# A diffusion-transformer layer on one core: x added by an accumulating DMA, token tiles 0 and 1 transposed together, narrow weight buffers in the down projection

## The chip, the cores and the metric

The kernel runs on one core of one Trainium2 chip. The metric is the device time of one execution in microseconds (us). Fewer is better.

## What is computed

One layer over 512 latent tokens of width 2048: a token mixer (mLSTM heads and differential attention heads, with 256 context tokens), its output projection, a normalised and gated residual, a modulated norm, and a gated feed-forward network of width 5632 with a width-3 convolution over the tokens. Cut to the part around the change:

```python
y_lat = jnp.concatenate([m_lat, d_lat], axis=-1) @ w_out[l]
x = x + ga1 * rmsnorm(y_lat, g_post_mix[l])

h_lat = modulate(rmsnorm(x, g_pre_ffn[l]), sh2, sc2)      # h * (1 + sc2) + sh2
x = x + ga2 * rmsnorm(conv_ffn(h_lat, w_up[l], conv_ffn_w[l], conv_ffn_b[l], w_down[l]), g_post_ffn[l])

def conv_ffn(h, w_up, conv_w, conv_b, w_down):
    u = dwconv3(h @ w_up, conv_w, conv_b)
    gate, val = jnp.split(u, 2, axis=-1)
    return (jax.nn.silu(gate) * val) @ w_down
```

## The kernel before

All data are float32. For TensorE each operand is split into a rounded high part and a low remainder (`split`: ScalarE casts the high part, VectorE subtracts), and each product is three matmuls (high by high, low by high, high by low). Weights come by DMA from SyncE's queue into `raw` tiles of 128x1024 (pool of three) and are split from there, either into "narrow" tiles `whi`/`wlo` of 128x512 (a pool of four of each, which is one block of weights) or into "wide" tiles `vhi`/`vlo` of 128x1024 (two of each, again one block).

The order of every engine is written out in the program and kept by the engine; nothing is chosen at run time. Where work is interleaved (deferred steps, generators), the builder's code sets that order.

**Output projection.** `phase_out_1` runs three of four groups of 512 input features with `nat_group`: for each block of 512 output columns (`cc`) the weights are split once, and four token tiles (`tt`) are multiplied by them. One `nat_unit` is one token tile by one block: 12 matmuls into one of two PSUM tiles named `nat`, then VectorE adds it into `y[tt][cc]` (L899). The fourth group is `nat_last`: all four blocks are split ahead, and token tile after token tile is finished. Behind each unit comes `each` (the sum of squares of y on ScalarE, L925, and the product with the gate row on VectorE, L978), behind each token tile comes `post`: sum, `pow` on GpSimd (L189), then y * rs + x (L990, x was loaded into a `raw` tile by L988 on SyncE's queue), the sum of squares of that (L925), the write of x to DRAM (`x1_d`, L992 on GpSimd's queue, 256 KB each), a second sum and `pow`, and the scaling by it (L997 on ScalarE, L999 on VectorE). In the trace the input tensor x appears as `in_xn`, the tiles as `xn`, and the DRAM tensor as `x_d`.

**Transposes and forms.** Token tile after token tile, four blocks of 128x128 are transposed on TensorE into one PSUM tile (`xt`, L71), shifted and scaled into `hf` by ScalarE (L1032, 128x128 each), and split into the operands of a Strassen-like up projection. Tiles 0 and 1 give the forms `A11` and `A12` (`put_form`, casts and subtractions on VectorE, L1065 and L1068); tiles 2 and 3 give `S1` to `S4` and `A22` (`sums`). `hf` of tiles 0 and 1 lies in tiles named `F` (five of them), which also hold up weights that are added by an accumulating DMA from GpSimd (`forms`, L1099). The transposes of the first two tiles stand between the last units of the output projection on TensorE where their data come in time.

**Up loop.** 44 steps `f`, each seven products of the Strassen form, with `up_first` of the first two steps among the transposes.

**Down projection.** 11 groups of four input blocks by four column blocks `cc`, again with `nat_group`. With `down=True` odd `cc` take the wide tiles and even `cc` the narrow ones, so that a block's weights can be split while the other pool's are in use. In each even `cc`, `step(64)` runs a piece of the modulation vectors for the second residual: two loads of 512 KB (`wmB`, L262) into `raw` tiles, and four VectorE operations on `macc` (L267, L269).

Of the kernel before, what the change touches and what calls it, by code (L numbers as in the profile page):

```python
# [58 lines left out]
class Prog:  # L59
# [40 lines left out]
    def load_w(self, src, n, act=False, wide=False):  # L100
# [4 lines left out]
        if wide:  # L105
            for j in range(n // 1024):
                raw = self.p_raw.tile([P, 1024], F32, tag="raw", name="raw")
                self.nc.sync.dma_start(raw, src[:, j * 1024:(j + 1) * 1024])
                hi, lo = self.wide_w()
                self.split(hi, lo, raw)  # L110
                for q in range(2):
                    his.append(hi[:, q * 512:(q + 1) * 512])
                    los.append(lo[:, q * 512:(q + 1) * 512])
            n = 0
# [786 lines left out]
    def nat_group(self, wsrc, acts, y, first, pool, tag, down=False):  # L901

        for cc in range(4):
            get = self.load_w(wsrc(cc), 2048, wide=down and cc % 2 == 1)
            if down and cc % 2 == 0:
                self.step(64)
            for tt in range(4):
                self.nat_unit(get, acts, tt, y, cc, first, pool, tag)
# [59 lines left out]
    def phase_out(self):  # L968
# [7 lines left out]
        def each(tt, cc):  # L976
            self.stat(ssy[tt], cc, y[tt][cc])
            nc.vector.tensor_tensor(y[tt][cc], y[tt][cc], rows[cc], ALU.mult)  # L978

        def post(tt):  # L980
# [3 lines left out]
            for cc in range(4):  # L984
                cs = slice(cc * 512, (cc + 1) * 512)
                if cc % 2 == 0:
                    x2 = self.p_raw.tile([P, 1024], F32, tag="raw", name="xn")
                    nc.sync.dma_start(x2, I["xn"][tt, :, cc * 512:(cc + 2) * 512])  # L988
                xn = x2[:, cc % 2 * 512:(cc % 2 + 1) * 512]
                nc.vector.scalar_tensor_tensor(xn, y[tt][cc], r, xn, ALU.mult, ALU.add)  # L990
                self.stat(ss, cc, xn)
                nc.gpsimd.dma_start(self.x1_d[tt, :, cs], xn)  # L992
                xs.append(xn)
            r2 = self.stat_done(ss)
# [11 lines left out]
        for n in ("A11", "A12", "A22"):  # L1006
            self.fm[n] = [[self.slot(n, F32R) for _ in range(4)] for _ in range(2)]
        hf = {}
        for tt in range(4):
# [3 lines left out]
            for cc in (0, 2, 1, 3):  # L1013
                if cc:
                    pt = self.ps_sm.tile([P, 512], F32, tag="sm", name="xt")
                else:
                    pt = self.ps_big.tile([P, 1024], F32, tag="big", name="xt")[:, :512]
                for j in range(4):
                    self.tr(pt[:, j * P:(j + 1) * P], y[tt][cc][:, j * P:(j + 1) * P], self.ident)
                if tt >= 2:  # L1020
                    h = self.u_tile("hf")
# [331 lines left out]
```

## Time and profile before

| what | value |
|---|---|
| time, median of 3 runs | 2743.49 us (2741.33 to 2744.75) |
| the profiled execution's own time | 2743.7 us |
| its span in the profile | 2741.9 us |
| TensorE busy | 2652.5 us, 97% of the span |
| VectorE busy | 1887.8 us, 69% |
| ScalarE busy | 1192.8 us, 44% |
| GpSimd busy | 178.6 us, 7% |
| bytes moved by DMA | 458.24 MB, 167 GB/s over the span |

The profile is of one execution; its times are microseconds from the start of the span. Busy time of an engine leaves out its waits and its DMA issues. In a row of the timeline the last bracket is the idle time before the instruction on its engine and what ended it; a row with x3 merges three alike, and its duration goes from the first's start to the last's end.

### The profile page before, as it was taken

To read this page: it belongs to the slowest core of one execution; us is meant where nothing else is said; L and a number is where in the kernel's file an instruction comes from. 1 tells how busy PE (TensorE), PEld (TensorE's weight loads), DVE (VectorE), ACT (ScalarE), POOL (GpSimd) and SP (SyncE) were. 2 spreads that over 40 slices of the span, in tenths; PEclk is the share of its full clock that TensorE was granted. 3 is DMA by queue.
4 is the path that set the end of the run, shared out by engine and by line. 5 is a ranking of instruction groups with operands and counts; after the bars stand their busy time and mean duration, and the time that the engine had idled before them with its cause. 6 is when DMAs were issued, how large, how long until landed. Compare 5 with 4: busy or idle time off the path is not lost.

```text
span 2741.9 us, 43239 instructions
## 1 busy us (share of the span) xinstructions
PE 2652.5 (97%) x16916; PEld 2355.4 (86%) x16916; DVE 1887.8 (69%) x3252; ACT 1192.8 (44%) x2185; POOL 178.6 (7%) x233
## 2 busy tenths in 40 slices
PE   6999999999999999999699999999999999999998
PEld 3678899888788888877699999999999988888786
DVE  6585867766656666546877777777777775666556
ACT  4242444434434343524755555555555563222222
POOL 0000000000000000001111111111111100000000
PEclk9999999999999999999899999999999999999999
DMA  8775434433433434344487777777777764544434
GB/s 280 273 242 196 133 117 138 138 110 115 125 136 100 154 109 132 100 139 154 131 226 197 202 193 200 192 205 196 200 197 199 204 220 159 176 160 142 135 106 151
DMA packets 139358, 458.24 MB, mean 167 GB/s; under 512 B 15936, under 2 KB 16352, under 8 KB 139152
## 3 DMA queue, kind: packets, MB, share of 16 engines
q1 hardware_dynamic: 119312, 386.64, 43.0%
q0 software_dynamic: 19840, 68.83, 11.8%
q8 instruction: 133, 2.18, 0.3%
q14 instruction: 73, 0.60, 0.1%
HBM read 429.10 MB, written 26.30 MB: 166 GB/s over the span
## 4 chain that ended last, share of the span: by engine, by line
PE 49%; DVE 1%; ACT 1%; DMA 1%; issue 0%; DVEq 0%; POOLq 0%; POOL 0%; ACTq 0%
PE up L68 31%; PE nat L68 18%; ACT hf L1032 1%; DMA raw<-in_wu 0%; DMA raw<-in_wmB 0%; DVE S L1068 0%; DVE vlo L144 0%; ACT junk L925 0%; ACT vhi L143 0%; DVE wlo L144 0%; PE xt L71 0%; PE modr L68 0%; ACT S L1067 0%; DVE A L1068 0%; DVE v L588 0%
## 5 line engine op out<-in xcount | busy, mean ns | idle before, releaser
L143 ACT CAST whi<-raw 128x512 fp32r<-128x512 f32 x492 | 302.8, 620 | 455.4 <-PE nat L68 174.6
L144 DVE TENSOR_TENSOR wlo<-raw,whi 128x512 fp32r<-128x512 f32 x492 | 337.4, 692 | 105.9 <-ACT whi L143 99.0
L68 PE MATMUL mm<-lhi,whi 128*128 128x512 f32 x912 | 373.5, 410 | 2.3 <-ACT whi L143 1.9
L68 PE MATMUL mm<-llo,whi 128*128 128x512 f32 x912 | 359.8, 395 | 0.0
L68 PE MATMUL mm<-lhi,wlo 128*128 128x512 f32 x912 | 359.8, 395 | 0.0
L68 PE MATMUL up<-S,whi 128*128 128x256 f32 x1408 | 259.3, 284 | 5.4 <-ACT S L1067 3.1
L269 DVE SCALAR_TENSOR_TENSOR macc<-raw,c,macc 128x512 f32<-128x512 f32 x240 | 179.6, 748 | 119.4 <-DMA raw<-in_wmB 116.9
L68 PE MATMUL up<-S,vhi 128*128 128x256 f32 x1408 | 253.8, 281 | 1.0 <-ACT val L1166 0.9
L899 DVE TENSOR_TENSOR y<-nat,y 128x512 f32<-128x512 f32 x208 | 142.8, 688 | 133.5 <-PE nat L68 132.6
L68 PEld LDWEIGHTS up<-S,whi 128*128 128x128 f32 x1408 | 220.0, 192 | 6.1 <-ACT S L1067 3.3
L68 PEld LDWEIGHTS up<-S,vhi 128*128 128x128 f32 x1408 | 215.5, 188 | 1.5 <-ACT val L1166 1.1
L68 PEld LDWEIGHTS mm<-lhi,whi 128*128 128x128 f32 x912 | 173.4, 190 | 41.1 <-issue 10.3
L68 PEld LDWEIGHTS mm<-lhi,wlo 128*128 128x128 f32 x912 | 172.3, 189 | 42.0 <-issue 3.3
L68 PE MATMUL up<-S,wlo 128*128 128x256 f32 x704 | 200.1, 284 | 2.3 <-DVE wlo L144 2.3
L68 PE MATMUL cx<-chl,whi 128*128 128x256 f32 x1056 | 199.4, 287 | 2.7 <-ACT vt L627 1.5
L68 PEld LDWEIGHTS mm<-llo,whi 128*128 128x128 f32 x912 | 173.0, 190 | 30.3 <-issue 3.4
L143 ACT CAST vhi<-raw 128x1024 fp32r<-128x1024 f32 x106 | 111.3, 1050 | 199.8 <-PE nat L68 154.8
L68 PE MATMUL up<-S,vlo 128*128 128x256 f32 x704 | 197.0, 280 | 0.0
L68 PE MATMUL up<-A,vhi 128*128 128x256 f32 x1056 | 192.9, 283 | 0.1
L68 PE MATMUL up<-A,whi 128*128 128x256 f32 x1056 | 192.8, 283 | 0.0
L68 PEld LDWEIGHTS cx<-chl,whi 128*128 128x128 f32 x1056 | 169.5, 192 | 10.1 <-ACT vt L627 2.4
L144 DVE TENSOR_TENSOR vlo<-raw,vhi 128x1024 fp32r<-128x1024 f32 x106 | 129.6, 1223 | 53.8 <-ACT vhi L143 53.6
(349 smaller groups left out, 5903.0 us busy)
## 6 DMA issues: line engine op xcount, KB each, us to landing
raw<-in_wu SPq DMA_DIRECT2D x132, 512.0 KB, 5.3
raw<-in_wmB SPq DMA_DIRECT2D x128, 512.0 KB, 3.9
raw<-in_w SPq DMA_DIRECT2D x105, 512.0 KB, 4.1
F<-in_wu SPq DMA_DIRECT2D x88, 512.0 KB, 5.0
F<-in_wu POOLq DMA_DIRECT2D x88, 512.0 KB, 7.6
raw<-in_wd SPq DMA_DIRECT2D x88, 512.0 KB, 4.5
mraw<-in_wmA SPq DMA_DIRECT2D x64, 512.0 KB, 5.7
raw<-in_wo SPq DMA_DIRECT2D x32, 512.0 KB, 4.0
```

The lines of the kernel that those rows point to most:

```text
L68: return self.pe(self.nc.tensor.matmul(*a, **k))
L143: self.nc.scalar.copy(hi, src)
L144: self.nc.vector.tensor_tensor(lo, src, hi.bitcast(F32), ALU.subtract)
L269: nc.vector.scalar_tensor_tensor(acc, r, c, acc, ALU.mult, ALU.add)
L899: nc.vector.tensor_tensor(y[tt][cc], ps, y[tt][cc], ALU.add)
L1032: nc.scalar.activation(h[:, js], pt[:, js], AF.Identity, bias=sh, scale=sc)
```

## The change

Three edits:

- For token tiles 0 to 2, `each` no longer multiplies y by the gate row; `post` does y * rs * row in one VectorE operation (L987 after) into the `raw` tile, a DMA from GpSimd's queue adds x to it in SBUF (L990 after, 512 KB each, two for a token tile), the sums of squares follow, and x is written to DRAM in 512 KB pieces (L993 after). Token tile 3 keeps the loads of x and the old arithmetic (L985 after).
- Token tiles 0 and 1 are transposed into shared PSUM tiles, block by block, after the last unit of the output projection. The shift takes 128x256 (both tiles at once), and the high parts of `A11` and `A12` are cast by ScalarE, 128x512 each, the low parts subtracted by VectorE, 128x512 each.
- `load_w` loses its wide form; the down projection uses the narrow tiles for every `cc`.

```diff
--- before.py
+++ after.py
@@ -97,21 +97,11 @@
     def slot(self, name, dt=F32):
         return self.p_slot.tile([P, 512], dt, tag="slot", name=name)
 
-    def load_w(self, src, n, act=False, wide=False):
+    def load_w(self, src, n, act=False):
 
         his, los = [], []
         if act:
             bh, bl = self.act("wact"), self.act("wact")
-        if wide:
-            for j in range(n // 1024):
-                raw = self.p_raw.tile([P, 1024], F32, tag="raw", name="raw")
-                self.nc.sync.dma_start(raw, src[:, j * 1024:(j + 1) * 1024])
-                hi, lo = self.wide_w()
-                self.split(hi, lo, raw)
-                for q in range(2):
-                    his.append(hi[:, q * 512:(q + 1) * 512])
-                    los.append(lo[:, q * 512:(q + 1) * 512])
-            n = 0
         for j in range(n // 512):
             if j % 2 == 0:
                 w = min(1024, n - j * 512)
@@ -901,7 +891,7 @@
     def nat_group(self, wsrc, acts, y, first, pool, tag, down=False):
 
         for cc in range(4):
-            get = self.load_w(wsrc(cc), 2048, wide=down and cc % 2 == 1)
+            get = self.load_w(wsrc(cc), 2048)
             if down and cc % 2 == 0:
                 self.step(64)
             for tt in range(4):
@@ -975,22 +965,32 @@
 
         def each(tt, cc):
             self.stat(ssy[tt], cc, y[tt][cc])
-            nc.vector.tensor_tensor(y[tt][cc], y[tt][cc], rows[cc], ALU.mult)
+            if tt == 3:
+                nc.vector.tensor_tensor(y[tt][cc], y[tt][cc], rows[cc], ALU.mult)
 
         def post(tt):
             r = self.stat_done(ssy[tt])
             ss = self.p_s.tile([P, 4], F32, tag="ssx", name="ssx")
             xs = []
             for cc in range(4):
-                cs = slice(cc * 512, (cc + 1) * 512)
                 if cc % 2 == 0:
                     x2 = self.p_raw.tile([P, 1024], F32, tag="raw", name="xn")
-                    nc.sync.dma_start(x2, I["xn"][tt, :, cc * 512:(cc + 2) * 512])
+                    ds = slice(cc * 512, (cc + 2) * 512)
+                    xd = I["xn"][tt, :, ds]
+                    if tt == 3:
+                        nc.sync.dma_start(x2, xd)
                 xn = x2[:, cc % 2 * 512:(cc % 2 + 1) * 512]
-                nc.vector.scalar_tensor_tensor(xn, y[tt][cc], r, xn, ALU.mult, ALU.add)
-                self.stat(ss, cc, xn)
-                nc.gpsimd.dma_start(self.x1_d[tt, :, cs], xn)
                 xs.append(xn)
+                if tt == 3:
+                    nc.vector.scalar_tensor_tensor(xn, y[tt][cc], r, xn, ALU.mult, ALU.add)
+                else:
+                    nc.vector.scalar_tensor_tensor(xn, y[tt][cc], r, rows[cc], ALU.mult, ALU.mult)
+                if cc % 2:
+                    if tt < 3:
+                        nc.gpsimd.dma_start(x2, xd, accum_op=ALU.add)
+                    for k in (cc - 1, cc):
+                        self.stat(ss, k, xs[k])
+                    nc.gpsimd.dma_start(self.x1_d[tt, :, ds], x2)
             r2 = self.stat_done(ss)
             for cc in range(4):
                 if cc % 2:
@@ -1005,35 +1005,44 @@
         self.fm = {}
         for n in ("A11", "A12", "A22"):
             self.fm[n] = [[self.slot(n, F32R) for _ in range(4)] for _ in range(2)]
+        def tr4(parts, name):
+            if name:
+                pt = self.ps_sm.tile([P, 512], F32, tag="sm", name="xt")
+            else:
+                pt = self.ps_big.tile([P, 1024], F32, tag="big", name="xt")[:, :512]
+            for j, (tt, cc, q) in enumerate(parts):
+                self.tr(pt[:, j * P:(j + 1) * P], y[tt][cc][:, q * P:(q + 1) * P], self.ident)
+            return pt
+
+        def shift(dst, src, k):
+            nc.scalar.activation(dst, src, AF.Identity, bias=self.mcol[:, 16 + k:17 + k],
+                                 scale=self.mcol[:, 32 + k:33 + k])
+
+
         hf = {}
-        for tt in range(4):
+        for cc in range(4):
+            h = self.f_tile("hf")
+            for half in range(2):
+                pt = tr4([(t, cc, 2 * half + q) for q in range(2) for t in range(2)], cc * 2 + half & 3)
+                for q in range(2):
+                    k = 2 * half + q
+                    shift(h[:, k * 256:(k + 1) * 256], pt[:, q * 256:(q + 1) * 256], cc * 4 + k)
+                hi, lo = (t[cc % 2 * 2 + half] for t in self.fm["A11" if cc < 2 else "A12"])
+                self.split(hi, lo, h[:, half * 512:(half + 1) * 512])
+            for tt in range(2):
+                hf[tt, cc] = h.rearrange("p (k t) -> p k t", t=256)[:, :, tt * P:(tt + 1) * P]
+        for tt in (2, 3):
             if tt == 2:
                 for n in ("S1", "S2", "S3", "S4"):
                     self.fm[n] = [self.act(n) for _ in range(2)]
             for cc in (0, 2, 1, 3):
-                if cc:
-                    pt = self.ps_sm.tile([P, 512], F32, tag="sm", name="xt")
-                else:
-                    pt = self.ps_big.tile([P, 1024], F32, tag="big", name="xt")[:, :512]
-                for j in range(4):
-                    self.tr(pt[:, j * P:(j + 1) * P], y[tt][cc][:, j * P:(j + 1) * P], self.ident)
-                if tt >= 2:
-                    h = self.u_tile("hf")
-                elif cc < 2:
-                    h2 = self.f_tile("hf")
-                    h = h2[:, :512]
-                else:
-                    h = h2[:, 512:]
-                hf[tt, cc] = h
-                for j in range(4):
-                    k = cc * 4 + j
-                    js = slice(j * P, (j + 1) * P)
-                    sh, sc = self.mcol[:, 16 + k:17 + k], self.mcol[:, 32 + k:33 + k]
-                    nc.scalar.activation(h[:, js], pt[:, js], AF.Identity, bias=sh, scale=sc)
-                if tt < 2:
-                    self.put_form("A11" if cc < 2 else "A12", cc % 2, tt, h, True)
-            if tt >= 2:
-                self.sums(tt, hf)
+                pt = tr4([(tt, cc, q) for q in range(4)], cc)
+                h = self.u_tile("hf")
+                for q in range(4):
+                    js = slice(q * P, (q + 1) * P)
+                    shift(h[:, js], pt[:, js], cc * 4 + q)
+                hf[tt, cc] = h.rearrange("p (k t) -> p k t", t=P)
+            self.sums(tt, hf)
             if tt == 2:
                 self.early = [self.up_first(0)]
             if tt == 3:
@@ -1050,7 +1059,7 @@
     def put_form(self, n, c, tt, src, on_dve=False):
 
         nc = self.nc
-        h3 = src.rearrange("p (a b) -> p a b", b=P)
+        h3 = src
         t0 = tt % 2 * P
         hi, lo = self.fm[n]
         if n[0] == "S":
@@ -1071,7 +1080,7 @@
         tt_ = self.nc.vector.tensor_tensor
         s1 = []
         for c in range(2):
-            s = self.slot("s1")
+            s = self.slot("s1").rearrange("p (k t) -> p k t", t=P)
             s1.append(s)
             tt_(s, hf[tt, c], hf[tt, c + 2], ALU.subtract)
             self.put_form("S1", c, tt, s, True)
```

How this moves instructions is shown at three places, in the order in which the engine takes them (the name of an instruction's output, `<-`, its inputs, and the shape; x3 stands for three alike in a row). Lines are those of the kernel in question; the changed kernel's are about ten lower.

GpSimd, at the end of the output projection, token tile 0 and the start of tile 1. `rs` is the small tile that `pow` works on. Before:

```order
L189 TENSOR_TENSOR rs_11974<-rs_11974,mhalf 128x1
L992 DMA x_d<-xn 128x512 x4
L189 TENSOR_TENSOR rs_11999<-rs_11999,mhalf 128x1
L189 TENSOR_TENSOR rs_12075<-rs_12075,mhalf 128x1
L992 DMA x_d<-xn 128x512 x4
```

And in the changed kernel:

```order
L179 TENSOR_TENSOR rs_11970<-rs_11970,mhalf 128x1
L990 DMA xn<-in_xn 128x1024 x2
L993 DMA x_d<-xn 128x1024 x2
L179 TENSOR_TENSOR rs_11993<-rs_11993,mhalf 128x1
L179 TENSOR_TENSOR rs_12065<-rs_12065,mhalf 128x1
```

The two accumulating loads stand between a token tile's first `pow` and its second, and the writes of x stand behind them.

VectorE, at the same place, token tile 1 and the first unit of tile 3. `ssx` holds the sums of squares of x, `ss` those of y. Before:

```order
L932 TENSOR_REDUCE rs_12075<-ss_11833 128x1
L188 TENSOR_SCALAR rs_12075<-rs_12075 128x1
L990 SCALAR_TENSOR_TENSOR xn<-y,rs_12075,xn 128x512 x4
L899 TENSOR_TENSOR y<-nat,y 128x512 x2
L932 TENSOR_REDUCE rs_12100<-ssx 128x1
L978 TENSOR_TENSOR y<-y,row 128x512
L188 TENSOR_SCALAR rs_12100<-rs_12100 128x1
L999 TENSOR_SCALAR y<-xn,rs_12100 128x512 x2
```

And in the changed kernel:

```order
L987 SCALAR_TENSOR_TENSOR xn<-y,rs_12065,row 128x512 x4
L889 TENSOR_TENSOR y<-nat,y 128x512 x3
L922 TENSOR_REDUCE rs_12088<-ssx 128x1
L178 TENSOR_SCALAR rs_12088<-rs_12088 128x1
L999 TENSOR_SCALAR y<-xn,rs_12088 128x512 x2
L889 TENSOR_TENSOR y<-nat,y 128x512
L922 TENSOR_REDUCE rs_12160<-ss_11834 128x1
```

The sum over `ssx`, which now comes after the accumulating loads, stands ahead of the sum over the next tile's `ss`, as it did before; one more unit's addition has moved ahead of it, and the products with the row are gone.

VectorE, in the down projection, about two blocks `cc`. `wlo` and `vlo` are the low parts of narrow and wide weights, `macc` the modulation piece, `glo` the low part of the next group's activations. Before:

```order
L899 TENSOR_TENSOR y<-nat,y 128x512
L269 SCALAR_TENSOR_TENSOR macc<-raw,c_95,macc 128x512
L899 TENSOR_TENSOR y<-nat,y 128x512
L269 SCALAR_TENSOR_TENSOR macc<-raw,c_95,macc 128x512
L144 TENSOR_TENSOR wlo<-raw,whi 128x512 x3
L899 TENSOR_TENSOR y<-nat,y 128x512
L144 TENSOR_TENSOR wlo<-raw,whi 128x512
L269 SCALAR_TENSOR_TENSOR macc<-raw,c_95,macc 128x512
L899 TENSOR_TENSOR y<-nat,y 128x512
L269 SCALAR_TENSOR_TENSOR macc<-raw,c_95,macc 128x512
L899 TENSOR_TENSOR y<-nat,y 128x512 x2
L144 TENSOR_TENSOR vlo<-raw,vhi 128x1024
```

And in the changed kernel:

```order
L134 TENSOR_TENSOR wlo<-raw,whi 128x512 x3
L889 TENSOR_TENSOR y<-nat,y 128x512
L134 TENSOR_TENSOR wlo<-raw,whi 128x512
L889 TENSOR_TENSOR y<-nat,y 128x512
L259 SCALAR_TENSOR_TENSOR macc<-raw,c_95,macc 128x512
L889 TENSOR_TENSOR y<-nat,y 128x512
L259 SCALAR_TENSOR_TENSOR macc<-raw,c_95,macc 128x512
L889 TENSOR_TENSOR y<-nat,y 128x512
L134 TENSOR_TENSOR wlo<-raw,whi 128x512 x2
L259 SCALAR_TENSOR_TENSOR macc<-raw,c_95,macc 128x512
L889 TENSOR_TENSOR y<-nat,y 128x512
L134 TENSOR_TENSOR wlo<-raw,whi 128x512 x2
```

The wide rows are gone, and in every second block a `macc` operation stands between the second and the third `wlo`.

## Rows read from the trace of the kernel before

**Rows 1.** Busy time by stage; columns: stretch, length, five engines, TensorE clock, DMA, GB/s.

```profile
1195.00:1255.00 60.00, 60.00 (x266) 49.47 (x265) 29.57 (x45) 14.55 (x24) 0.00 (x0) 1.00 0.28 90
1268.00:1316.40 48.40, 45.84 (x205) 37.21 (x204) 36.51 (x69) 29.24 (x76) 10.41 (x18) 1.00 0.48 167
1316.40:1371.00 54.60, 34.62 (x204) 30.67 (x202) 51.04 (x106) 43.45 (x105) 6.22 (x9) 0.75 0.41 116
2235.00:2700.00 465.00, 460.63 (x2008) 374.87 (x2007) 271.18 (x379) 127.21 (x178) 1.06 (x2) 1.00 0.46 152
```

**Rows 2.** Who waited for whom, 1255 to 1375; columns: total us, times, longest.

```profile
PE xt L71 <- ACT hf L1032: 13.9, 8, 5.7
```

**Rows 3.** Timeline of VectorE at the end of the output projection.

```profile
1281.40 0.15 DVE L932 TENSOR_REDUCE rs<-ss 128x1 f32<-128x4 f32 x1
...
1282.43 2.74 DVE L990 SCALAR_TENSOR_TENSOR xn<-y,rs,xn 128x512 f32<-128x512 f32 x4 [0.69 <-POOL rs L189]
...
1318.20 0.69 DVE L978 TENSOR_TENSOR y<-y,row 128x512 f32<-128x512 f32 x1 [0.98 <-ACT junk L925]
...
1319.88 2.74 DVE L990 SCALAR_TENSOR_TENSOR xn<-y,rs,xn 128x512 f32<-128x512 f32 x4 [0.72 <-POOL rs L189]
```

**Rows 4.** Timeline of ScalarE at the same place and behind it.

```profile
1283.21 0.63 ACT L925 ACTIVATE junk<-xn 128x512 f32<-128x512 f32 x1 [2.46 <-DVE xn L990]
1283.75 0.19 ACT L925 ACTIVATION_READ_ACCUMULATOR junk<-xn 128x1 f32 x1
...
1288.39 1.34 ACT L997 ACTIVATE y<-xn,rs 128x512 f32<-128x512 f32 x2 [1.24 <-POOL rs L189]
...
1326.20 4.63 ACT L1032 ACTIVATE hf<-xt,mcol 128x128 f32<-128x128 f32 x13
1330.66 1.11 ACT L143 CAST vhi<-raw 128x1024 fp32r<-128x1024 f32 x1
...
1344.63 1.21 ACT L1067 CAST S<-s 128x512 fp32r<-128x512 f32 x2
```

**Rows 5.** DMA issues of the whole span; last column: median us to landing.

```profile
raw<-in_wmB SPq DMA_DIRECT2D x128, 512.0 KB, 3.9
...
F<-in_wu SPq DMA_DIRECT2D x88, 512.0 KB, 5.0
F<-in_wu POOLq DMA_DIRECT2D x88, 512.0 KB, 7.6
```

**Rows 6.** DMA issues from 1160 to 1330, same columns.

```profile
xn<-in_xn SPq DMA_DIRECT2D x8, 512.0 KB, 4.4
...
F<-in_wu POOLq DMA_DIRECT2D x2, 512.0 KB, 10.0
```

**Rows 7.** Timeline of VectorE: a block change in the output projection, then one in the down projection.

```profile
1221.96 2.05 DVE L144 TENSOR_TENSOR wlo<-raw,whi 128x512 fp32r<-128x512 f32 x3 [0.64 <-ACT whi L143]
...
2314.85 1.37 DVE L144 TENSOR_TENSOR wlo<-raw,whi 128x512 fp32r<-128x512 f32 x2 [0.65 <-ACT whi L143]
2316.90 0.75 DVE L269 SCALAR_TENSOR_TENSOR macc<-raw,c,macc 128x512 f32<-128x512 f32 x1 [0.68 <-DMA raw<-in_wmB]
...
2318.17 1.28 DVE L144 TENSOR_TENSOR wlo<-raw,whi 128x512 fp32r<-128x512 f32 x2
```

**Rows 8.** Timeline of SyncE's queue, then of VectorE, in the down projection.

```profile
2420.63 0.33 SPq L262 DMA_DIRECT2D raw<-in_wmB  x1
...
2426.18 0.75 DVE L269 SCALAR_TENSOR_TENSOR macc<-raw,c,macc 128x512 f32<-128x512 f32 x1 [3.17 <-DMA raw<-in_wmB]
```

**Rows 9.** Timeline of TensorE: two idle stretches of about two us.

```profile
2238.11 0.51 PE L68 MATMUL nat<-whi,ghi 128*128 128x512 f32 x1 [1.69 <-ACT whi L143]
...
2575.43 0.28 PE L71 MATMUL modr<-tabs,mcol 128*16 128x128 f32 x1 [2.08 <-DVE mcol L286]
```

**Rows 10.** Busy time by stretch behind these two; columns as in rows 1.

```profile
2576.00:2579.50 3.50, 3.50 (x10) 2.74 (x9) 0.02 (x1) 0.00 (x0) 0.52 (x1) 0.53 0.58 183
2239.00:2243.00 4.00, 3.79 (x16) 2.99 (x17) 4.00 (x7) 2.73 (x4) 0.00 (x0) 1.00 0.55 201
```

## The prediction, made before the changed kernel was run

> **What bounds the kernel now.** I read the busy time by stage first. In the output projection up to its last group and in the down projection TensorE is busy in 60.00 of 60.00 us and in 460.63 of 465 us [rows 1]: nothing else costs time there as long as its work stays beside the matmuls. In the last group (1268 to 1316) it is busy in 45.84 of 48.40 us, so the finishing of token tiles on the other engines just keeps up. Only from 1316.4 to 1371 does TensorE stand idle, 20 of 54.6 us, with the clock at 0.75 on the mean and VectorE busy in 51.04 us. The waits of TensorE name the main releaser there: ScalarE's shift `hf`, 13.9 us [rows 2]. So the change touches three places: a stage that just keeps up, a stage that is bound by VectorE and ScalarE, and a stage that is bound by TensorE alone. 0.2% of the time, 5.5 us, is about what a measurement can tell from no change.
>
> **The end of the output projection.** Before, token tile t starts its y * rs + x operation at 1282.43 for the first and at 1319.88 for the last [rows 3]: 37.45 us for three tiles, 12.5 each, set mostly by the matmuls.
>
> Removed: 12 products with the row at 0.69 us [rows 3], 8.3 us of VectorE, six loads of x on SyncE's queue, and the many 256 KB writes on GpSimd's queue become eight of 512 KB. Before, these products lie beside matmuls (all but the one ahead of each sum), so I cost the removal at 0.5 us once, at the first tile. The freed SyncE queue makes weights arrive earlier, which nobody waits for.
>
> Added: the statistics of x wait until the accumulating load has landed. Behind that wait stand, on ScalarE, the statistics of the next tile's y, and on VectorE the sum over `ssx`, the scaling, and only then the next tile's last addition and its sum. Both engines keep their order, so the load's whole landing time enters the chain from one tile to the next, which becomes: four y * rs * row operations, 2.74 us [rows 3]; the landing of the second load; the two statistics that hang on it, 2 x 0.73 us (0.63 and the read of the sum, which ends 0.73 behind the start [rows 4]); reduction, `pow` and scaling until the next operation starts, 1.03 us (from 1281.40 to 1282.43 [rows 3]); two scalings on ScalarE, 1.34 us, that stand ahead of the next tile's remaining statistics [rows 4]; three of these, 2.19 us; and 1.03 us again for sum and `pow`. Without the landing this is 9.8 us.
>
> The landing has no row of its own. The nearest is the same kind of DMA of the same size, on the same queue: the accumulating load of up weights, 7.6 us by its median over the span [rows 5]. A plain load to the same tiles lands in 5.0 us, one of x in 4.4 us, and the two accumulating loads just ahead of this place took 10.0 us [rows 5, 6]. I take 7.6, for this is a median of 88 with a second load beside it as here, and keep 5.0 and 10.0 as ends. The Trainium skill prices the queue at less: "DMA: Bandwidth & Descriptors", section "SWDGE vs HWDGE vs iDMA" and its table of specifications, give about 1 us to the first byte from GpSimd's queue and about 0.6 us from SyncE's, 0.4 apart; the load of x would then land in about 4.8 us (an estimate from that page and the row of x), and the sum below would be 8 us smaller. The rows have 2.6 us between the two queues for the same bytes, and they decide.
>
> So a tile takes 9.8 + 7.6 = 17.4 us, and three take 52.2 instead of 37.45: the last tile starts 14.7 us later, plus about 0.7 for its four products in a row, minus the 0.5 above: **+15 us** (+7 at a landing of 5.0, +22 at 10.0). TensorE cannot fill this: it has two PSUM tiles, and their additions wait on VectorE in the same order. GpSimd's second `pow` waits behind the writes of x, which wait for the same landing and issue while ScalarE does its statistics; costed at 0. SyncE's weight loads are early.
>
> **Transposes and forms.** Before, ScalarE needs from 1319.88 to 1330.66, 10.8 us, until it casts the first up weight [rows 3, 4]. On this way the change puts six casts of 128x512 that VectorE did before, 0.6 us each from the row of two in 1.21 [rows 4], 3.6 us; eight shifts of 128x256 and eight of 128x128 stand where there were sixteen of 128x128 at 4.63 / 13 = 0.36 us [rows 4], about 0.1 more for each of the wide ones, 0.8 us. Some 1.4 us of the casts fit into the wait for the last `pow`. Net **+3 us**. VectorE loses some 5 us of casts in this stage, and it is the busier engine; but it now waits for ScalarE's casts, and its list behind the first up weight is the same within a few us. I cost that at 0 with 5 us either way. What is saved by the joint shift (sixteen calls instead of 32) lies mostly in the wait for the loads, where it is worth nothing.
>
> **The down projection.** Without the wide pool, a block's weights can be cast only as the last token tile of the block before releases them, one after the other. That alone is what the output projection does at each block, at full TensorE busy [rows 1]; there three `wlo` take 2.05 us in one go [rows 7], which is the pace of the matmuls (266 matmuls began in those 60 us, so the 12 of a unit take 2.71 us for four pieces of the weights). So most block changes cost nothing. But at 13 of the 44 blocks the new order has a `macc` operation and an addition between the second and the third `wlo`, and that `macc` waits for the load of its second piece. This pattern stands twice in the order before, and one of them can be read: two `wlo` from 2314.85 to 2316.22, then 0.68 us of waiting for the `wmB` load, the `macc` at 2316.90, an addition, and the other two at 2318.17 [rows 7]. In one go the third would have started at about 2316.1, so it is 2.07 us late. Before, this is covered, for TensorE is then on a wide block whose weights were ready. In the changed kernel it is not covered. The `raw` buffers make the delay about the same there: the first `wmB` load gets its buffer from the last `wlo` of the block ahead, the second from the first `macc` pair, so two landings of 3.9 us [rows 5] follow one another in a block of 4 x 2.71 = 10.8 us. With some 0.1 us of slack, 13 x 2.0 = **+26 us**. Ends: if the load has landed, `macc` and half of the addition alone are worth some 0.6, 13 x 0.6 = 8 us; if one of the two loads takes as long as the one issued at 2420.63 whose `macc` started at 2426.18, 5.55 us [rows 8], 13 x 3.65 = 47 us.
>
> **Sum.** 2743.7 (the profiled execution's own time) + 15 + 3 + 26 = 2787.7 us. That execution was 0.2 us above the median of the runs, so the prediction is **2787.5 us**.
>
> **Rivals.**
> - *The clock falls at each new idle.* Behind the idle of 2.08 us at 2575.43 TensorE ran at 0.53 for 3.5 us, behind that of 1.69 us at 2238.11 at 1.00 [rows 9, 10]. The stalls of 2.0 us lie between. 0.53 is all but the lower of the clock's two levels (1.2 of 2.4 GHz), and 3.5 x 0.47 = 1.6 us of work were lost. If each of the 13 stalls pays that, it is 21 us more: 2808 us. Against it: in the changed kernel a stall comes in the middle of dense matmuls, as at 2238. [...] Chance 0.15.
> - *The down projection keeps its cover.* If the loads of `macc` come early enough and VectorE catches up within a unit, as it does at the plain block changes, only the first two terms are left: 2743.5 + 18 = 2761.5 us. Against it: the row of 2314.85, where the wait was there with the same buffers. Chance 0.12.
> - *Faster.* In the stage from 1316.4 TensorE waits 13.9 us for `hf` [rows 2]. The joint shift and the split on two engines take VectorE's casts away (5 us) and ten or so calls from ScalarE. That shows if the last tile starts no later than before; it needs a landing of 7.6 - 15 / 3 = 2.6 us or less, and a down projection that is covered: then about 2743.5 - 7 = 2736 us. Against it: no 512 KB load in these rows has a median under 3.9 us. Chance 0.04.
> - *The terms cancel or the waits are not there*, within 5.5 us of before: it would take both a landing under about 3 us and no late `wlo`. Chance 0.03.
>
> **How the numbers follow.** The forecast has what is left, 0.66. Its lowest ends together make 2743.5 + 7 + 3 - 5 + 8 = 2756.5, its highest 2743.5 + 22 + 3 + 5 + 47 = 2820.5. Both at one end is unlikely, so the range goes from 2764 (it leaves out the rival with one term) to 2815 (it takes in the clock rival). Faster by over 0.2%: 0.04; within: 0.03; slower: 0.93.
>
> **What would show it.** Right: the y * rs operations of the tiles start 17 to 18 us apart; ScalarE's first statistic of x waits some 7 us for a DMA, three times; TensorE waits for VectorE's `y` in 1290 to 1335 by some 15 us in all; the first cast `vhi` comes at about 1349; in the down projection some 26 us of idle TensorE in pieces of about 2 us, ended by `wlo`, with `macc` waiting for `wmB` ahead of it; the up loop is unchanged at 864 us. Wrong: tiles 12 to 13 us apart, or a down projection with TensorE busy in all but 5 us, or its clock under 0.95 there.

## The result, and the profile after

The changed kernel takes 2814.74 us (median of four runs, 2806.75 to 2819.94) against 2743.26 us: a ratio of 1.0263 (95% interval 1.0249 to 1.0277), some 72 us slower. The forecast was 2787.5 us, with a range up to 2815. The median lies 0.3 us inside that end, and 1.0263 times the 2743.5 us that the forecast started from is 2815.6, just beyond it: a loss of 72 us where 44 were forecast. The profiled execution of the changed kernel took 2816.99 us with a span of 2815.2.

The busy time by stage, as in [rows 1]; the stages lie later now. The third stretch ends in the first steps of the up loop, the last covers most of the down projection:

```profile
1195.00:1255.00 60.00, 60.00 (x266) 49.45 (x265) 31.06 (x47) 15.48 (x25) 0.00 (x0) 1.00 0.30 97
1268.00:1332.20 64.20, 48.49 (x205) 38.76 (x203) 29.54 (x59) 26.27 (x71) 12.54 (x19) 0.89 0.48 130
1332.20:1396.00 63.80, 39.75 (x227) 34.74 (x227) 48.36 (x80) 46.31 (x102) 4.88 (x6) 0.70 0.35 107
2254.40:2750.00 495.60, 453.05 (x1917) 367.16 (x1915) 259.94 (x394) 124.92 (x198) 1.06 (x2) 0.96 0.41 135
```

The last group of the output projection keeps TensorE busy in 48.49 of 64.20 us where it was 45.84 of 48.40. In the down projection 42.6 us of 495.6 are now idle, and the clock is at 0.96.

**Token tile to token tile.** VectorE's timeline of the changed kernel, the operations that answer to [rows 3]:

```profile
1279.74 2.74 DVE L987 SCALAR_TENSOR_TENSOR xn<-y,rs,row 128x512 f32<-128x512 f32 x4 [0.69 <-POOL rs L179]
...
1297.10 2.74 DVE L987 SCALAR_TENSOR_TENSOR xn<-y,rs,row 128x512 f32<-128x512 f32 x4 [0.72 <-POOL rs L179]
...
1314.92 2.74 DVE L987 SCALAR_TENSOR_TENSOR xn<-y,rs,row 128x512 f32<-128x512 f32 x4 [0.72 <-POOL rs L179]
...
1332.23 2.74 DVE L985 SCALAR_TENSOR_TENSOR xn<-y,rs,xn 128x512 f32<-128x512 f32 x4 [0.72 <-POOL rs L179]
```

They are 17.36, 17.82 and 17.31 us apart, 52.5 us in all where it was 37.45. ScalarE shows what it waited for (its timeline, first token tile):

```profile
1287.07 0.63 ACT L915 ACTIVATE junk<-xn 128x512 f32<-128x512 f32 x1 [8.39 <-DMA xn<-in_xn]
...
1289.95 0.63 ACT L915 ACTIVATE junk<-xn 128x512 f32<-128x512 f32 x1 [1.55 <-DMA xn<-in_xn]
```

The first statistic waits 8.39 us for the accumulating load, the third 1.55 us for the second load. The DMA issues of the whole span have the load itself, the last column being us to landing; the plain load of the last tile stands below it:

```profile
xn<-in_xn POOLq DMA_DIRECT2D x6, 512.0 KB, 6.5
...
xn<-in_xn SPq DMA_DIRECT2D x2, 512.0 KB, 3.8
```

**The down projection.** Its TensorE waits, 2254.4 to 2750 (us in total, times, longest):

```profile
PE nat L68 <- DVE wlo L134: 20.4, 13, 2.5
PE modr L68 <- DVE macc L259: 19.6, 4, 5.0
PE nat L68 <- ACT whi L133: 1.0, 1, 1.0
PE modr L71 <- DVE mcol L276: 0.5, 1, 0.5
```

There are 13 waits for `wlo`, as many as were forecast, but not all at the forecast places. By its order in the trace VectorE takes a `macc` and an addition between the second and the third `wlo` at twelve places. At eight of these TensorE waits for `wlo`, 1.1 to 2.5 us, 1.86 on the mean; the other five waits for `wlo`, 5.5 us in all, lie elsewhere, three of them in the first blocks of the stage, where the order differs. At the other four places stands a wait of nearly 5 us that the prediction does not have: the `modr` matmuls, which turn a finished `macc` into columns, wait for its last operation, and every matmul behind them in TensorE's order waits too. VectorE's timeline ahead of the first of these four waits, and then TensorE's:

```profile
2322.49 0.75 DVE L259 SCALAR_TENSOR_TENSOR macc<-raw,c,macc 128x512 f32<-128x512 f32 x1 [3.20 <-DMA raw<-in_wmB]
...
2325.38 1.37 DVE L134 TENSOR_TENSOR wlo<-raw,whi 128x512 fp32r<-128x512 f32 x2 [0.28 <-ACT whi L133]
2328.41 0.75 DVE L259 SCALAR_TENSOR_TENSOR macc<-raw,c,macc 128x512 f32<-128x512 f32 x1 [1.65 <-DMA raw<-in_wmB]
2329.08 0.68 DVE L889 TENSOR_TENSOR y<-nat,y 128x512 f32<-128x512 f32 x1
2329.68 1.28 DVE L134 TENSOR_TENSOR wlo<-raw,whi 128x512 fp32r<-128x512 f32 x2
2330.88 0.74 DVE L259 SCALAR_TENSOR_TENSOR macc<-raw,c,macc 128x512 f32<-128x512 f32 x1
...
2331.68 1.87 PE L68 MATMUL modr<-tabs,macc 128*128 128x1 f32 x8 [4.95 <-DVE macc L259]
```

At the next of the twelve places no `modr` matmul stands, and TensorE waits for the third `wlo` instead (VectorE's timeline, then TensorE's):

```profile
2359.88 0.75 DVE L259 SCALAR_TENSOR_TENSOR macc<-raw,c,macc 128x512 f32<-128x512 f32 x1 [1.63 <-DMA raw<-in_wmB]
...
2361.15 1.28 DVE L134 TENSOR_TENSOR wlo<-raw,whi 128x512 fp32r<-128x512 f32 x2
...
2361.89 0.50 PE L68 MATMUL nat<-wlo,ghi 128*128 128x512 f32 x1 [1.62 <-DVE wlo L134]
```

Two `wmB` landings follow one another, 3.20 and 1.65 us of VectorE waiting; the second stands between `wlo` two and three, as at 2314.85 before [rows 7], and the last `macc` ends behind all four `wlo`.

Where the 73.3 us between the two profiled spans lie: the first tile's start -2.7 (TensorE stood at half clock from 1183.6 for 6.8 us in the profile of before, and not in this one; the program is the same up to there, and in the four runs below with narrow tiles alone this start lies anywhere from 1280.05 to 1286.18), the three tile steps +15.0, from there to the first up weight 14.0 us instead of 10.8, +3.2, from that weight to the first matmul of the down projection +4.1, from its first matmul to the last of the span's `nat` matmuls 550.2 instead of 496.2, +54.0, the rest -0.3.

### The profile page after: what moved, and what is told of

Read it like the earlier page. It is cut to its first block, busy times and chain, and to the rows that moved or that the text cites. A ratio compares the mean times of both kernels' runs of the same rounds, so it can differ in the third digit from the quotient of the medians.

```text
span 2815.2 us, 43285 instructions
## 1 busy us (share of the span) xinstructions
PE 2672.8 (95%) x16916; PEld 2367.5 (84%) x16916; DVE 1880.5 (67%) x3256; ACT 1200.0 (43%) x2217; POOL 180.3 (6%) x231
## 4 chain that ended last, share of the span: by engine, by line
PE 64%; DMA 8%; DVE 7%; issue 5%; ACT 3%; POOL 1%; SPq 0%; DVEq 0%; POOLq 0%; ACTq 0%
PE up L68 31%; PE mm L68 12%; PE nat L68 11%; DMA raw<-in_wmB 6%; PE cx L68 5%; DVE wlo L134 2%; DVE macc L259 2%; PE do L68 1%; PE sc L68 1%; ACT whi L133 1%; DVE y L889 1%; DMA xn<-in_xn 1%; PE pt L71 1%; PE o L68 1%; DMA F<-in_wu 1%
## 5 line engine op out<-in xcount | busy, mean ns | idle before, releaser
L133 ACT CAST whi<-raw 128x512 fp32r<-128x512 f32 x572 | 352.2, 620 | 664.1 <-PE nat L68 374.0
L134 DVE TENSOR_TENSOR wlo<-raw,whi 128x512 fp32r<-128x512 f32 x572 | 390.5, 690 | 133.8 <-ACT whi L133 128.2
L68 PE MATMUL nat<-wlo,ghi 128*128 128x512 f32 x640 | 256.1, 401 | 20.6 <-DVE wlo L134 20.6
L68 PE MATMUL nat<-whi,ghi 128*128 128x512 f32 x640 | 254.3, 400 | 2.4 <-ACT whi L133 2.4
L68 PE MATMUL nat<-whi,glo 128*128 128x512 f32 x640 | 253.1, 398 | 0.0
```

Of the source, the lines that this page charges most:

```text
L68: return self.pe(self.nc.tensor.matmul(*a, **k))
L133: self.nc.scalar.copy(hi, src)
L134: self.nc.vector.tensor_tensor(lo, src, hi.bitcast(F32), ALU.subtract)
```

## The experiments

Each run is set against runs of the kernel before on the same chip. Ratios are to it; the us behind a ratio are what the ratio makes of 2743.3.

**One part at a time.** In the first run the wide tiles are put back into the changed kernel; the other three each put one part into the kernel before.

```diff
-            get = self.load_w(wsrc(cc), 2048)
+            get = self.load_w(wsrc(cc), 2048, wide=down and cc % 2 == 1)
```

> The changed kernel with the wide weight tiles back in the down projection. Theory (the two losses add, and the down projection's belongs to the narrow tiles alone): the down projection begins about 20 us later than before and takes as long as before, 2764 us (2760 to 2768), the clock at 1.00 in the down projection. Rival (what happens ahead disturbs the down projection too): over 2775 us.

Measured: 1.0086 (1.0069 to 1.0103), +24 us. The tiles start at 1280.1 to 1332.2 as in the changed kernel, and the down projection takes 497.4 us from its first matmul to the last `nat` (before: 496.2), the clock being at half for 6.8 us of it. What happens ahead does not disturb it.

```diff
-            get = self.load_w(wsrc(cc), 2048, wide=down and cc % 2 == 1)
+            get = self.load_w(wsrc(cc), 2048, wide=False)
```

> The kernel before with narrow tiles alone. Theory: the down projection loses by itself about 50 us, 2793 us (2786 to 2800): some 20 us of idle TensorE ended by wlo, some 20 us by macc ahead of the modr matmuls, the rest at half clock. Rival (it is the order that the other edits bring that costs): under 2760 us.

Measured: 1.0166 (1.0151 to 1.0181), +46 us; the down projection takes 542.0 us. The waits of its TensorE, 2240 to 2710:

```profile
PE modr L68 <- DVE macc L269: 18.7, 4, 5.1
PE nat L68 <- DVE wlo L144: 17.9, 12, 2.3
```

The narrow tiles bring both waits by themselves.

```diff
-                    nc.sync.dma_start(x2, I["xn"][tt, :, cc * 512:(cc + 2) * 512])
...
+                    if tt < 3:
+                        nc.gpsimd.dma_start(x2, xd, accum_op=ALU.add)
```

(and the rest of `each` and `post` as in the change)

> The kernel before with the accumulating load alone; transposes as before. Theory (the landing is in the chain from tile to tile): token tiles 17 to 18 us apart as in the changed kernel, 2757 us (2753 to 2765). Rival (the loss there belongs to the joint transposes, which all stand behind the last unit): within 5 us of 2743.

Measured: 1.0061 (1.0046 to 1.0076), +17 us. The tiles start at 1281.65, 1298.88, 1316.45 and 1334.55: 17.2 to 18.1 us apart without any joint transposes.

The last of the four takes the transposes and splits of the change and leaves `each` and `post` as they were:

```diff
-        for tt in range(4):
+        for cc in range(4):
+            h = self.f_tile("hf")
+            for half in range(2):
+                pt = tr4([(t, cc, 2 * half + q) for q in range(2) for t in range(2)], cc * 2 + half & 3)
```

> The kernel before with the joint transposes, shifts and splits alone; x loaded and added as before. Theory: token tiles 12.5 us apart as before; ScalarE has 3 us more ahead of the first up weight, VectorE 5 us less behind it: 2740 to 2750 us. Rival (moving the transposes behind the last unit is what costs): 2758 us or more.

Measured: 1.0020 (1.0010 to 1.0030), +5.5 us, in the upper half of what the theory had. The tiles are 12.4 to 12.7 us apart. From the last tile's start to the first matmul of the down projection it is 922.2 us, where it was 915.0: the 5 us less of VectorE's time behind the first up weight did not show. So the joint transposes cost something, and 17 + 5.5 + 46 = 68 of the 72 us come from the parts alone.

**Why the narrow tiles cost.** Three runs with narrow tiles alone. The first moves the `modr` matmuls one block later:

```diff
-                self.defer(12, lambda q=q, cc=cc, acc=acc: self.modb_cols(q, cc, acc))
+                if self.pin:
+                    self.defer(12, lambda q=q, cc=cc, acc=acc: self.modb_cols(q, cc, acc))
+                else:
+                    self.late = lambda q=q, cc=cc, acc=acc: self.modb_cols(q, cc, acc)
...
+            if down and cc == 3 and self.late:
+                self.late, fn = None, self.late
+                fn()
```

> Narrow tiles alone, with the four groups of modr matmuls (and what hangs on them) moved one block of columns, some 11 us, later. Theory (TensorE waits in order for macc, whose loads come late, and its clock falls behind these waits of nearly 5 us): the 18.7 us of modr waits go, and with them most of the half clock: 2788 - 19 - 8 = 2761 us (2755 to 2768); the wlo waits stay. Rival (the loads of macc are the bound, and the wait comes back at another place): 2780 us or more.

Measured: 1.0086 (1.0071 to 1.0101), +24 us, 22 less than narrow tiles alone. The `modr` waits are gone, and so is most of the half clock (10.2 us of it in the down projection where the run before had 34.1); the `wlo` waits grew. Its TensorE waits, 2240 to 2710:

```profile
PE nat L69 <- DVE wlo L145: 25.1, 16, 2.5
```

So some of the `modr` waits came back as `wlo` waits, as the rival had it, but a smaller part. The four places where `modr` waited now have waits for `wlo`, 7.4 us in all (TensorE's timeline):

```profile
2316.23 0.50 PE L69 MATMUL nat<-wlo,ghi 128*128 128x512 f32 x1 [1.72 <-DVE wlo L145]
...
2410.85 0.50 PE L69 MATMUL nat<-wlo,ghi 128*128 128x512 f32 x1 [1.63 <-DVE wlo L145]
...
2509.07 0.50 PE L69 MATMUL nat<-wlo,ghi 128*128 128x512 f32 x1 [2.08 <-DVE wlo L145]
...
2605.62 0.50 PE L69 MATMUL nat<-wlo,ghi 128*128 128x512 f32 x1 [1.93 <-DVE wlo L145]
```

Of the time that the `modr` waits took, this much would have been lost there in any case. The next run leaves out most of the `macc` work:

```diff
+                        if self.nstep > 48 and kg + j > 0:
+                            continue
```

> Narrow tiles alone, where each piece of four loads pairs in the down projection keeps only the first macc operation and its load (it leaves out 60 of 64 macc operations and 28 of 32 wmB loads there). Theory (narrow tiles cost nothing where no macc stands between): under 4 us of waits beyond those of before, 2743 to 2749 us. Rival (narrow tiles stall at each block by themselves, or half the clock's loss is theirs): 2760 us or more.

Measured: 0.9982 (0.9968 to 0.9996). The waits for `wlo` are down to this (TensorE's waits, 2240 to 2710), and narrow tiles as such cost nothing that can be told:

```profile
PE nat L68 <- DVE wlo L144: 0.8, 3, 0.3
```

This run leaves out the loads as well as VectorE's work. The next one keeps all of both and only spreads them:

```diff
+                        if self.nstep > 48 and j == 1:
+                            yield
...
-            if down and cc % 2 == 0:
-                self.step(64)
+            if down:
+                self.step(80)
```

> Narrow tiles alone, with the macc work of the down projection spread: one wmB load with its two macc operations in every block, in place of two loads and four operations in every second block. The work is the same. Theory (two wmB landings in a row behind a block's last wlo make the third and fourth wlo and the modr matmuls late): the waits for wlo and for macc fall below 10 us in all, 2750 us (2743 to 2760). Rival (any macc among narrow tiles costs, by VectorE's time): 2770 us or more.

Measured: 1.0006 (0.9997 to 1.0016), the time of before within what can be told. The waits, and VectorE's timeline at one block change:

```profile
PE nat L68 <- DVE wlo L144: 3.8, 5, 1.4
PE modr L71 <- DVE mcol L288: 1.4, 1, 1.4
```

```profile
2310.29 0.75 DVE L269 SCALAR_TENSOR_TENSOR macc<-raw,c,macc 128x512 f32<-128x512 f32 x1 [3.58 <-DMA raw<-in_wmB]
2310.95 0.68 DVE L901 TENSOR_TENSOR y<-nat,y 128x512 f32<-128x512 f32 x1
2311.56 0.74 DVE L269 SCALAR_TENSOR_TENSOR macc<-raw,c,macc 128x512 f32<-128x512 f32 x1
...
2312.82 2.03 DVE L144 TENSOR_TENSOR wlo<-raw,whi 128x512 fp32r<-128x512 f32 x3
```

VectorE still waits 3.58 us for a `wmB` load, but in the middle of a block, and the `wlo` go in one piece. The loss of the narrow tiles was the bunching of two loads and their four operations in every second block, not the buffers' width and not the sum of VectorE's time. Whether the loads or the operations alone have to be spread was not tried.

**Why the accumulating load costs.** The load alone, with the half of `post` that needs it put behind the next tile:

```diff
+            held.append((tt, xs, xt))
+            if tt:
+                post2(*held.pop(0))
+            if tt == 3:
+                post2(*held.pop(0))
+
+        def post2(tt, xs, xt):
+            ss = self.p_s.tile([P, 4], F32, tag="ssx", name="ssx")
```

> The accumulating load alone, with the statistics, the write and the scaling of a token tile put behind the next tile's y * rs * row operations (tile 1's x lies in F tiles, so that the buffers suffice). Theory (the landing counts because the next tile's work stands behind it in order): tiles 11 to 13 us apart, 2743 us (2737 to 2749). Rival (the landing counts in any order, or the load disturbs others): 2753 us or more.

Measured: 1.0010 (1.0001 to 1.0019), +3 us where the load alone had +17. VectorE's timeline, the starts of the tiles:

```profile
1274.34 2.74 DVE L999 SCALAR_TENSOR_TENSOR xn<-y,rs,row 128x512 f32<-128x512 f32 x4 [0.66 <-POOL rs L189]
...
1286.01 2.74 DVE L999 SCALAR_TENSOR_TENSOR xn<-y,rs,row 128x512 f32<-128x512 f32 x4 [0.68 <-POOL rs L189]
...
1299.23 2.74 DVE L999 SCALAR_TENSOR_TENSOR xn<-y,rs,row 128x512 f32<-128x512 f32 x4 [2.16 <-POOL rs L189]
...
1313.12 1.41 DVE L997 SCALAR_TENSOR_TENSOR xn<-y,rs,xn 128x512 f32<-128x512 f32 x2 [2.00 <-POOL rs L189]
...
1321.10 1.41 DVE L997 SCALAR_TENSOR_TENSOR xn<-y,rs,xn 128x512 f32<-128x512 f32 x2 [4.19 <-DMA xn<-in_xn]
```

They are 11.7, 13.2 and, to the last tile, 13.9 us apart, though the accumulating loads landed no sooner (7.4 us by their median, 6.5 in the run with the load alone). From tile to tile it was the load's place in the order that cost. The total says less. The last tile now waits in its middle for its plain load of x, which lands in 6.8 us (3.6 in the run with the load alone), so that from its start to the first up weight it is 17.7 us (before: 10.8). Against that the first tile starts 8.1 us earlier than before: the first loads into F tiles, which in the run with the load alone are issued from 1165 to 1176, here go out between 1263 and 1299. The two nearly cancel, which was not forecast, and whether the moved loads are what makes the start earlier was not tried.

**What the joint transposes cost.** One guess was the buffers: ScalarE's shift of the fourth block waits 0.52 us at 1341.54 for `vlo`, which holds an F tile, and all sums follow. A sixth F tile has no room as the pools stand (another pool wants 49.4 KB per partition, and 48.4 would be left), so a small attention tile moves to another pool. Here it is as a control in the kernel before, and then with the joint transposes:

```diff
-        return self.p_x.tile([P, 1024], F32, tag="F", name=name, bufs=5)
+        return self.p_x.tile([P, 1024], F32, tag="F", name=name, bufs=6)
-            low[t, c] = self.p_s.tile([P, P], F32R, tag="ql", name="ql", bufs=3)
+            low[t, c] = self.p_at1.tile([P, P], F32R, tag="ql", name="ql", bufs=3)
```

> The kernel before with the sixth F tile alone, as a control for the last one. Theory: the wait of 4.7 us at 1343 for hf has the same cause, 2738 us (2735 to 2742). Rival: that wait has another cause, within 2 us of before.

Measured: 0.9994 (0.9985 to 1.0004), as the rival had it. The wait of 4.7 us is gone all the same, and waits for `vhi`, `vlo` and `wlo` of 3.5 to 4.0 us stand in its place.

> The joint transposes alone, with a sixth F tile (room for it by moving a small attention tile to another pool). Theory (the shift of the fourth block waits for an F tile that an up weight holds, and all sums behind it are late): the wait of 9.5 us of TensorE for hf shrinks to under 4 us, ratio to before 0.998 (0.996 to 1.000). Rival (the loss is the order and ScalarE's casts): ratio 1.001 or more.

Measured: 1.0021 (1.0010 to 1.0032), the same as with five. The wait of 9.5 us is gone from the trace, and waits for `vhi`, `vlo` and `wlo` of 3.5 to 4.8 us stand in its place, since the order changed with the buffers. The guess falls as an explanation of the loss. A run with this, the accumulating load and the late statistics together (wide tiles in the down projection) was expected at 2737 us (2730 to 2744), with a rival of 2748 or more, that the late statistics leave ScalarE and VectorE more to do behind the last unit. It measured 1.0028 (1.0017 to 1.0038), +8 us, as the rival had it and about what the two parts lose one by one (3 and 6). Then the transposes and shifts were put ahead:

```diff
+            if tt == 2:
+                early()
```

(`early` holds the transposes and shifts of tiles 0 and 1, in `post`; the splits stay behind)

> The joint transposes alone with six F tiles, but the transposes and shifts of tiles 0 and 1 are put behind token tile 2's work, ahead of the last four units of the output projection; the splits stay where they were. Theory (the joint transposes cost because the shifts that lay beside the matmuls of the output projection now all stand behind them): at least 16 shifts ahead of the last tile's y * rs + x operation, where the run without this had 9, and the ratio to before falls to 0.999 (0.996 to 1.001). Rival (ScalarE's casts and the late sums cost, wherever the transposes are): ratio 1.002 or more.

Measured: 0.9992 (0.9983 to 1.0001); the interval lies apart from the one of the run without this. The shifts that ScalarE starts up to 1317, in the view of the tile `hf`, first with the joint transposes alone:

```profile
L1018 ACT ACTIVATE hf<-xt,mcol x9: 548/565/586, 1306.2 to 1315.4; 128x256 f32<-128x256 f32 x9
```

and in this run, where the last tile also starts at 1315.4:

```profile
L990 ACT ACTIVATE hf<-xt,mcol x25: 447/552/592, 1295.1 to 1314.6; 128x256 f32<-128x256 f32 x16, 128x128 f32<-128x128 f32 x9
```

25 shifts instead of 9 lie beside the output projection (the run with six F tiles has nine, too). That the place of the shifts is what costs agrees with it; the order of the rest changed as well, and 2.9 us of the difference between the two profiles with six F tiles lie already in the first tile's start (1276.24 and 1273.31), so this is one consistent run more than a proof. No version that does all the work was faster than the kernel before by more than can be measured.

**The changed kernel, mended.** First the `macc` work spread, then the statistics late as well (both edits as above).

> The changed kernel whole, with the macc work spread over all blocks of the down projection and nothing else. Theory (the narrow tiles' loss is the bunched macc work alone): as the run without narrow tiles, ratio to before 1.0086 (1.006 to 1.011). Rival (narrow tiles lose something else when the stage begins later): 1.015 or more.

Measured: 1.0105 (1.0090 to 1.0121). The waits for `wlo` in the down projection fall to 2.2 us, those of `modr` for `macc` are gone.

> The changed kernel whole, with the macc work spread and the statistics of x behind the next tile's work. Theory (with both losses mended the cost of the joint transposes is left): ratio to before 1.003 (1.000 to 1.005). Rival (the accumulating load costs with the joint transposes what it does not cost alone): 1.006 or more.

Measured: 1.0025 (1.0014 to 1.0036): +7 us are left of 72, about what the joint transposes cost alone. Its first tile, too, starts early, at 1273.73.

## Why the prediction was wrong, and where it was right

The step that failed is the term of the down projection: 26 us were forecast and 54 measured. The prediction followed the late `macc` to VectorE's next instructions, and not to TensorE, where the `modr` matmuls wait for its result; and it left the clock out of the sum, as a rival with a chance of 0.15. The runs show both in its place: four waits of 4.8 to 5.0 us for `macc`, and 47.8 us at half clock.

- *The chain from tile to tile, 17.4 us.* Right: 17.36, 17.82, 17.31; three steps of 52.5 us where 52.2 were written. The landing in it was sized at 7.6 us, and the load's own median is 6.5; the second load is issued 0.54 us behind the last y * rs * row operation, since GpSimd was still issuing the first (0.89 us from 1281.69), which the sum did not have. The two errors cancel in part, which is luck. The run with late statistics shows that from tile to tile the mechanism is the order. One sign was off: TensorE waits for `y` not some 15 us in 1290 to 1335 but 6.7, and 8.5 at once for `hf`, the joint transposes standing behind the last unit.
- *ScalarE until the first up weight, +3 us.* The size is right: 14.0 us instead of 10.8. With the joint transposes alone it is 12.2, so the six casts do not cost this by themselves.
- *Behind it, 0 with 5 us either way.* +4.1 us in the changed kernel, within the bound but not 0; the joint transposes alone have +7 from the last tile's start on. The joint shift was taken to save only time that is worth nothing. The run with the shifts put ahead agrees with another reading, that the 16 shifts which the kernel before has beside the last units had to be done later, but it does not prove it.
- *The down projection, 26 us.* This term is wrong: 54 us. Its own mechanism, the third `wlo` behind a `macc`, was sized about right: 2.0 us forecast for a place, 1.86 measured at the eight places where it can be seen. At the other four `modr` waits for the same late `macc`, 4.9 us a time, 19.6 in all. By the run with `modr` one block later about 7.4 us of these would have been waits for `wlo` anyway, so the forecast mechanism comes to some 28 us (20.4 + 7.4) and the reader on TensorE adds some 12; both are estimates, for that run has narrow tiles alone. The prediction had asked of the added wait what stands behind it on its own engine, and not who reads its result. The rest of the 54, once the idle time that before had there (4.4 us) is taken off the 42.6, is 54.0 - 38.2 = 15.8 us, which go with the half clock: 47.8 us of it from the first matmul of the stage to its last.
- *The rival of the clock.* It came in part, and mostly behind the waits that were not forecast: 34.1 of the 47.8 us stand at the four `modr` waits. With narrow tiles alone, moving the `modr` matmuls took away two thirds of the half clock.
- *The down projection keeps its cover* and *faster* did not come; the first is what the spread `macc` work shows is possible.

## What to carry to other kernels

When an operation gets later, list everyone who reads its result, on every engine, before pricing the delay: the reader that stands in the bounding engine's order costs more than the neighbours on the late engine. A DMA that is put into the middle of a chain costs its whole landing time if the next tile's work stands behind its consumer in order; with that consumer one tile later the tiles here were 11.7 to 13.9 us apart instead of 17.2 to 18.1. A pool that is just large enough loses to bunched side work; the same work spread evenly can cost nothing.

## What the runs showed of the hardware

Not every idle stretch of TensorE lowered its clock. In the changed kernel's down projection the granted clock was at half behind all four waits of 4.8 to 5.0 us, and behind only three of the 13 for `wlo`: those of 1.90, 2.47 and 2.52 us, but not one of 1.93. Busy time by stretch behind the wait of 1.93 us at 2281.59, behind the first `modr` wait, behind that of 2.47 us at 2489.59, and near the end of the stage:

```profile
2281.60:2285.00 3.40, 3.40 (x15) 2.69 (x16) 1.80 (x3) 0.59 (x1) 0.00 (x0) 1.00 0.59 192
2333.40:2339.00 5.60, 5.60 (x14) 4.44 (x15) 0.42 (x3) 0.00 (x0) 0.00 (x0) 0.50 0.34 130
2489.60:2492.60 3.00, 3.00 (x7) 2.42 (x8) 1.67 (x3) 0.00 (x0) 0.00 (x0) 0.50 0.45 119
2752.30:2755.60 3.30, 3.30 (x9) 2.61 (x8) 1.65 (x3) 1.53 (x4) 0.00 (x0) 0.50 0.87 288
```

The last row stands behind a wait of 1.43 us for `whi` at 2750.28. So the length of a single wait does not sort the short ones.

The Trainium skill's "TensorE: Matmul & The Clock Gate", section "HAM oscillation", describes a kernel whose clock falls again at each of its waits for data, all of them longer than the short ones here; for the four long waits the trace agrees.

The accumulating load of x from GpSimd's queue landed in 6.5 us and the plain one of the same size from SyncE's queue in 3.8 us, 2.7 apart, about as wide as between the two kinds of up weights before [rows 5]. The Trainium skill's "DMA: Bandwidth & Descriptors", section "Specifications", gives about 1 us and about 0.6 us to the first byte of the two queues, 0.4 apart. The measurement decides, and what the accumulation itself has of the difference was not tried.
